# A hybrid decoder step: the sample scan's eight states in one run of TensorE passes

## The chip, the cores and the metric

The program runs on one core of one Trainium2 chip. The metric is the device time of one execution in microseconds (us): 2281.77 us before the change, the median of three runs (2281.49 to 2285.34). The engines are named as in the profile: PE is TensorE, PEld its loading of stationary operands, DVE is VectorE, ACT is ScalarE, POOL is GpSimd; SP is SyncE, which here only issues transfers.

## The reference

One inference step of a decoder layer: a SwiGLU feed-forward, a mixer, and a second feed-forward, each between RMS norms. It treats a prompt of 256 tokens with a zero initial state, and a sample group of eight sequences of four tokens, each with a stored state. The mixer has 4 GLA heads (128 keys, 256 values) and 8 HGRN heads (128 keys, 128 values). Both kinds are this recurrence, in chunks with exact causality:

```
decay  = where(causal, exp(cum_t - cum_s), 0)
scores = sum_d(q_t * k_s * decay)
o      = scores @ v + (q * exp(cum)) @ s
s_new  = exp(last) * s + (k * exp(last - cum)).T @ v
```

So a sample's output `o` has two parts: the sample's own scores times its own values, and its decayed queries times the stored state `s`. The updated states are outputs too.

## The kernel before, in words

All activations lie with features on partitions, 288 token columns to a tile: 256 of the prompt and 32 of the sample (8 sequences of 4 tokens). Weights come from HBM in units of 128x1024 floats on the SP queue (class `Weights`, lines 62 and 64), and ACT and DVE split each into a rounded part and a remainder (lines 96 and 97). Each 128x128 block of weights then makes three matmuls of 288 columns (lines 548 to 550). `block` runs through such products for 16 feature tiles `k`, and after every `k` it calls a `tick`.

The scans of the mixer live in these ticks. There are six: two for GLA and four for HGRN, with two heads each. Each is a generator (`scan`); a tick runs it on to its next `yield`, so that every step's instructions stand between the products of a weight block. The instructions of an engine keep the order that the program's planner writes out, which follows the order in the code but may move an instruction whose inputs it expects late.

A scan has nine steps (`LEVELS` + 1) that build the scores of the prompt in `Dg` and `X`, and those of the sample in `Ds` (32x32, zero between sequences). Step 3 also writes `qm[a]`: for each sequence b a block of 32 columns, which holds its four decayed queries in their places among the sample's 32 tokens and zeros elsewhere. Then come, for each head `a`:

- `out(a)`, line 1158: the prompt's output into the PSUM tile `o` (lines 1165 to 1167), three plain float32 matmuls for each 128 values; and the own-score part of the sample into the PSUM tile `os` (line 1169), values stationary (128x128) and the 32 columns of `Ds` streamed, into columns beyond the first 256.
- `sample(a, b0)`, line 1183, once for each load of states: four calls for a GLA head (`nb` = 2 sequences a load), two for an HGRN head (`nb` = 4). It computes the new states' increment in the PSUM tile `sn` (line 1191 or 1194), multiplies `qm` with each stored state (line 1198: stationary operand of 128x32, the state streamed, 256 or 128 columns) into one quarter of 32 partitions of `os`, chosen by b % 4, updates the state in place on DVE (line 1202) and stores it on POOL's queue (line 1204).
- `inter_a`, `inter_b`: the four quarters of `os` are copied to `it` and summed, turned, onto the own-score columns with the selection matrix `sel` (lines 1209 and 1214); then `norm_a` to `norm_c`.

Stored states come in through `load_state` (line 934), 256 KB a load, on the SP queue between the weights: one call in each of the steps 5 to 8 and one at the start of every `sample`. A GLA scan has eight loads, an HGRN scan four. The loads share five buffers (`bufs=5`); a buffer is free again once its updated state has been stored.

Of the kernel before, what the change touches and what calls it, by code (L numbers as in the profile page):

```python
# [9 lines left out]
F32 = mybir.dt.float32  # L10
# [6 lines left out]
P = 128  # L17
TP = 256
TS = 32
T = TP + TS  # L20
NB = 8
# [7 lines left out]
LEVELS = 8  # L29
# [96 lines left out]
def trunk_kernel(ctx, tc, x_prompt, x_sample, state_gla, state_hgrn, norm_gains, f1_in, f1_out, f2_in, f2_out,  # L126
# [3 lines left out]
    V, S, G, PE = nc.vector, nc.scalar, nc.gpsimd, nc.tensor  # L130
# [36 lines left out]
    def auxtile(name):  # L167
        return aux.tile([P, 512], F32, name=name, tag="aux")
# [607 lines left out]
    def mixer(pn, border):  # L776
        with ExitStack() as mx:
# [4 lines left out]
            sp = []  # L782
# [15 lines left out]
            its, vs32, qm = [], [], []  # L798
# [7 lines left out]
            Ds = cst.tile([P, 2, TS], F32, name="Ds")  # L806
# [48 lines left out]
            def halves(t, h, right):  # L855

                v = t[:, :, 0:T if h <= 2 else TP].rearrange("p a (n two k) -> p a n two k", two=2, k=h)
                return v[:, :, :, 1 if right else 0, :]
# [51 lines left out]
            def scan(d, Vt, V32, Vs, gla, ytile0, s0, sp_out, ss_out):  # L910
# [3 lines left out]
                dv = 256 if gla else 128  # L914
                nv = dv // P
                nb = 512 // dv
# [3 lines left out]
                fs, c = [d["f"]], 0  # L920
# [6 lines left out]
                states = {}  # L927

                def load_state():
                    if loads:  # L930
                        a, b0 = loads.pop(0)
                        t = sp[0].tile([P, nb, dv], F32, name="s0", tag="s0", bufs=5)
                        with tc.issue_after(W.last[W.loaded - 3]):
                            nc.sync.dma_start(t, s0[b0:b0 + nb, a].rearrange("b p v -> p b v"))
                        states[a, b0] = t
# [12 lines left out]
                def lay(lv, src):  # L948
                    h = 1 << lv
                    S.activation(R[:, :, lv, :].rearrange("p a (n k) -> p a n k", k=h), halves(src, h, True), AF.Copy)  # L950
# [52 lines left out]
                def update(lv, keys=None):  # L1003

                    h = 1 << lv
                    n = (T if h <= 2 else TP) // (2 * h)
                    f = fs[lv][:, :, 0:2 * n].rearrange("p a (n two) -> p a n two", two=2)
                    left, right = f[:, :, :, 0:1], f[:, :, :, 1:2]
                    if h < P and not keys:
                        v = halves(Q, h, True)  # L1010
                        V.tensor_tensor(v, v, left.broadcast_to(v.shape), op=ALU.mult)
                    if keys is not False:
                        v = halves(k, h, False)
                        V.tensor_tensor(v, v, right.broadcast_to(v.shape), op=ALU.mult)
                    if h < P and not keys:
                        V.tensor_tensor(fs[lv + 1].unsqueeze(3), left, right, op=ALU.mult)
# [12 lines left out]
                def score23():  # L1029
                    pss = [auxtile("sc23_0"), mmtile("sc23_1")]  # L1030
                    for i in range(2):
                        for a in range(2):
                            PE.matmul(pss[i][:, a * 192:(a + 1) * 192], k[:, a, i * P:(i + 1) * P],
                                      R2[0][:, :, a, i * 64:(i + 1) * 64], start=a == 0, stop=True,
                                      skip_group_check=True)
                    return pss
# [55 lines left out]
                for step in range(LEVELS + 1):  # L1092
                    if step == 0:
                        V.scalar_tensor_tensor(own.unsqueeze(3), halves(q, 1, False), 128.0, halves(k, 1, False),
                                               op0=ALU.mult, op1=ALU.mult)
                        S.activation(oh, rp, AF.Copy)
                        V.tensor_tensor(Q, q, d["f"], op=ALU.mult)
                        V.tensor_tensor(ol, rp, oh.bitcast(F32), op=ALU.subtract)
                        lay(0, q)
                    elif step == 1:  # L1100
                        update(0)
                        lay(1, Q)
                    elif step == 2:
                        pss[1] = score01()
                        update(1)
                        lay23(0)
                    elif step == 3:
                        puts = put01(*pss.pop(1))
                        update(2, False)
                        ready = lay23(1)  # L1110
                        with tc.issue_after(ready):
                            puts.pop(0)()
                    else:
                        pss[step - 1] = score23() if step == 4 else score(step - 1)
                        if step == 4:
                            update(2, True)
                        elif step == 5:
                            put23(*pss.pop(3))
                        else:
                            put(step - 2, pss.pop(step - 2))  # L1120
                        update(step - 1)
                        if puts:
                            with tc.issue_after(ready):
                                puts.pop(0)()
                    if step == 3:
                        for a in range(2):

                            S.activation(qm[a].rearrange("p (b c) -> p b c", c=TS + ST)[:, :, 0:ST],
                                         Q[:, a, TP:T].rearrange("p (b t) -> p b t", t=ST), AF.Copy)
                            S.activation(K3[:, a], k[:, a, TP:T].unsqueeze(1).broadcast_to([P, 3, TS]), AF.Copy)  # L1130
                    if step >= LEVELS - 3:
                        load_state()
                    yield
                put(LEVELS - 1, pss.pop(LEVELS - 1))
                kds, bds, sqs, pos, mss = {}, {}, {}, {}, {}
# [22 lines left out]
                def out(a):  # L1158
                    vc = Vt[:, :, a * dv:(a + 1) * dv]

                    po, ss = auxtile("o"), auxtile("os")
                    for j in range(nv):
                        vj = vc[:, :, j * P:(j + 1) * P]
                        c0, c1, c2 = j * TP, j * TP + P, (j + 1) * TP
                        PE.matmul(po[:, c0:c1], vj[:, 0, :], Dg[:, 0, a, :], start=j == 0, stop=True, skip_group_check=True)
                        PE.matmul(po[:, c1:c2], vj[:, 0, :], X[:, a, :], start=False, stop=False, skip_group_check=True)
                        PE.matmul(po[:, c1:c2], vj[:, 1, :], Dg[:, 1, a, :], start=False, stop=True, skip_group_check=True)
                        c0 = TP + j * TS
                        PE.matmul(ss[:, c0:c0 + TS], V32[:, a * dv + j * P:a * dv + (j + 1) * P], Ds[:, a, :],
                                  start=j == 0, stop=False, skip_group_check=True)  # L1170
                    pos[a] = po, ss

                def final(a):
# [9 lines left out]
                def sample(a, b0):  # L1183

                    load_state()
                    s = states.pop((a, b0))
                    ks, bd = kds[a][1], bds.pop((a, b0))
                    ps = auxtile("sn")
                    if gla:
                        for i in range(nb):  # L1190
                            PE.matmul(ps[:, i * dv:(i + 1) * dv], bd[:, i, :], Vs[:, a * dv:(a + 1) * dv],
                                      start=i == 0, stop=True, skip_group_check=True)
                    else:
                        PE.matmul(ps, ks, bd.rearrange("p b c -> p (b c)"), start=True, stop=True)
                    for i in range(nb):
                        b = b0 + i
                        r = slice(b % 4 * TS, (b % 4 + 1) * TS)
                        PE.matmul(pos[a][1][r, 0:dv], qm[a][:, b * TS:(b + 1) * TS], s[:, i, :],
                                  start=False, stop=b >= NB - 4, skip_group_check=True)
                    for i in range(nb):  # L1200
                        b = b0 + i
                        V.scalar_tensor_tensor(s[:, i, :], s[:, i, :], fs[2][:, a, 64 + b:65 + b],
                                               ps[:, i * dv:(i + 1) * dv], op0=ALU.mult, op1=ALU.add)
                    G.dma_start(ss_out[b0:b0 + nb, a].rearrange("b p v -> p b v"), s)
# [178 lines left out]
            for kind, g in HORDER:  # L1383
# [8 lines left out]
                for j in list(ds):  # L1392
                    if j // 2 in vts:
                        c = slice((j % 2) * 256, (j % 2 + 1) * 256)
# [116 lines left out]
```

## Time and profile before

| | |
|---|---|
| median of the runs | 2281.77 us |
| profiled execution | 2281.72 us, its span 2279.5 us |
| PE busy | 2265.8 us, 99% of the span |
| DVE, ACT, POOL busy | 1397.6, 1015.4, 134.6 us |
| granted clock of TensorE | 0.998 |
| DMA | 382.43 MB, mean 168 GB/s |

The scans stand in the span between about 913 and 1290 us. In the views, a row of a timeline gives the start in us from the span's start, the duration, engine, line, operation, the tiles written and read, the sizes, and how many instructions are put together in the row. A matmul `128*32 128x256` has a stationary operand of 128 rows by 32 columns and streams 256 columns. The recorded durations of matmuls overlap, since the array is pipelined. A plain float32 matmul shows as two instructions; the fp32r ones of the weight products show as one.

### The profile page before, as it was taken

How to read it: one execution, taken by the hardware profiler on the slowest of the kernel's cores; microseconds unless marked ns; L12 is line 12 of the kernel's file. 1: busy time of each engine (PE TensorE's matmuls, PEld its weight loads, DVE VectorE, ACT ScalarE, POOL GpSimd, SP SyncE). 2: the span in 40 equal slices, each digit the busy share in tenths (PEclk: the TensorE clock that was granted, in tenths of full speed). 3: DMA queues.
4: the chain of work that ended last, by engine and by line, in shares of the span. 5: the costliest groups of instructions: out<-in, count | busy, mean ns of one | idle time of the engine just before them, and what ended most of it. 6: DMA issues, size and time to landing. Idle time of an engine off the chain costs nothing.

```text
span 2279.5 us, 42047 instructions
## 1 busy us (share of the span) xinstructions
PE 2265.8 (99%) x17216; PEld 2240.5 (98%) x17216; DVE 1397.6 (61%) x2293; ACT 1015.4 (45%) x1539; POOL 134.6 (6%) x241
## 2 busy tenths in 40 slices
PE   9999999999999999999999999999999999999998
PEld 9999999999999999999999999999999999999998
DVE  7545545554555468778878754954555455545546
ACT  6443333333334346555556654644333333333344
POOL 2000000000000002001000000340000000000005
PEclk9999999999999999999999999999999999999999
DMA  7555555445555544556565554565555555455445
GB/s 218 169 167 166 167 167 165 166 165 166 166 165 184 167 158 148 165 160 186 156 172 169 160 185 158 157 191 166 167 167 166 167 167 165 164 168 165 165 164 157
DMA packets 225601, 382.43 MB, mean 168 GB/s; under 512 B 20242, under 2 KB 60224, under 8 KB 225408
## 3 DMA queue, kind: packets, MB, share of 16 engines
q1 hardware_dynamic: 214736, 365.15, 49.9%
q0 software_dynamic: 8496, 14.41, 2.3%
q8 instruction: 135, 2.21, 0.4%
q10 hardware_dynamic: 2176, 0.18, 0.1%
q14 instruction: 58, 0.48, 0.1%
HBM read 363.75 MB, written 11.80 MB: 165 GB/s over the span
## 4 chain that ended last, share of the span: by engine, by line
PE 97%; DVE 1%; ACT 0%; issue 0%; DMA 0%; DVEq 0%; SPq 0%; POOL 0%; ACTq 0%; POOLq 0%
PE gate L548 10%; PE gate L550 10%; PE gate L549 10%; PE up L550 8%; PE up L548 8%; PE up L549 8%; PE out L549 8%; PE out L550 8%; PE out L548 8%; PE mo L550 1%; PE hfq L548 1%; PE mo L548 1%; PE mo L549 1%; PE hfq L549 1%; PE hfq L550 1%; PE hi L548 1%
## 5 line engine op out<-in xcount | busy, mean ns | idle before, releaser
L97 DVE TENSOR_TENSOR wl<-raw,wh 128x1024 fp32r<-128x1024 f32 (+1 forms) x674 | 821.5, 1219 | 631.4 <-ACT wh L96 627.1
L96 ACT ACTIVATE wh<-raw 128x1024 fp32r<-128x1024 f32 (+1 forms) x674 | 711.8, 1057 | 1036.1 <-PE gate L549 318.1
L550 PE MATMUL gate<-xh,wl 128*128 128x288 f32 x1660 | 489.1, 295 | 0.5 <-DVE wl L97 0.5
L548 PE MATMUL gate<-xh,wh 128*128 128x288 f32 x1660 | 489.1, 296 | 0.1
L549 PE MATMUL gate<-xl,wh 128*128 128x288 f32 x1660 | 485.8, 295 | 0.4 <-DVE xl L255 0.4
L549 PE MATMUL out<-hl,wh 128*128 128x288 f32 x1408 | 415.6, 295 | 0.0
L550 PE MATMUL up<-xh,wl 128*128 128x288 f32 x1408 | 415.1, 295 | 0.0
L550 PE MATMUL out<-hh,wl 128*128 128x288 f32 x1408 | 415.0, 295 | 0.0
L548 PE MATMUL up<-xh,wh 128*128 128x288 f32 x1408 | 414.8, 295 | 0.0
L549 PE MATMUL up<-xl,wh 128*128 128x288 f32 x1408 | 414.6, 294 | 0.0
L548 PE MATMUL out<-hh,wh 128*128 128x288 f32 x1408 | 413.8, 294 | 0.3 <-DVE u L626 0.3
L548 PEld LDWEIGHTS gate<-xh,wh 128*128 128x128 f32 x1660 | 310.9, 188 | 1.9 <-issue 1.0
L550 PEld LDWEIGHTS gate<-xh,wl 128*128 128x128 f32 x1660 | 311.6, 188 | 1.1 <-DVE wl L97 1.0
L549 PEld LDWEIGHTS gate<-xl,wh 128*128 128x128 f32 x1660 | 310.4, 188 | 0.9 <-DVE xl L255 0.6
L548 PEld LDWEIGHTS out<-hh,wh 128*128 128x128 f32 x1408 | 264.6, 188 | 0.6 <-DVE u L626 0.6
L550 PEld LDWEIGHTS out<-hh,wl 128*128 128x128 f32 x1408 | 264.7, 188 | 0.0
L548 PEld LDWEIGHTS up<-xh,wh 128*128 128x128 f32 x1408 | 264.1, 188 | 0.4 <-ACT g L618 0.3
L549 PEld LDWEIGHTS out<-hl,wh 128*128 128x128 f32 x1408 | 264.4, 188 | 0.0
L549 PEld LDWEIGHTS up<-xl,wh 128*128 128x128 f32 x1408 | 264.2, 188 | 0.1
L550 PEld LDWEIGHTS up<-xh,wl 128*128 128x128 f32 x1408 | 264.2, 188 | 0.0
L706 DVE TENSOR_TENSOR y<-out,y 128x288 f32<-128x288 f32 x288 | 121.0, 451 | 101.3 <-PE out L550 98.3
L548 PE MATMUL hfq<-xh,wh 128*128 128x288 f32 x256 | 78.1, 305 | 0.0
(382 smaller groups left out, 2544.0 us busy)
## 6 DMA issues: line engine op xcount, KB each, us to landing
raw<-in_ffn_w_in_dram SPq DMA_DIRECT2D x351, 512.0 KB, 3.4
raw<-in_ffn_w_out_dram SPq DMA_DIRECT2D x176, 512.0 KB, 3.5
raw<-in_mix_w_in_dram SPq DMA_DIRECT2D x64, 512.0 KB, 3.7
raw<-in_mix_w_in_dram SPq DMA_DIRECT2D x96, 256.0 KB, 3.1
raw<-in_mix_w_out_dram SPq DMA_DIRECT2D x32, 512.0 KB, 3.6
out_dram<-s POOLq DMA_DIRECT2D x32, 256.0 KB, 3.1
s<-in_state_gla_dram SPq DMA_DIRECT2D x16, 256.0 KB, 4.1
s<-in_state_hgrn_dram SPq DMA_DIRECT2D x16, 256.0 KB, 5.0
```

The costliest lines, as they stand in the source:

```text
L96: i1 = self.nc.scalar.activation(h[:, c], raw[:, c], AF.Copy).ins
L97: i2 = self.nc.vector.tensor_tensor(l[:, c], raw[:, c], h[:, c].bitcast(F32), op=ALU.subtract).ins
L548: yield lambda: PE.matmul(dst, w[0][:, c:c + P], parts[0], start=start, stop=False)
L549: yield lambda: PE.matmul(dst, w[0][:, c:c + P], parts[1], start=False, stop=False)
L550: yield lambda: PE.matmul(dst, w[1][:, c:c + P], parts[0], start=False, stop=stop)
L706: V.tensor_tensor(y[k], ps, y[k], op=ALU.add)
```

## The change

All products of `qm` with the stored states move from `sample` to `out`: the eight states of a head stand one behind the other, right behind the prompt's output. The own-score product is turned round: `Ds[:, a, :]` (32 columns) is the stationary operand now and the sample's values are streamed, a quarter of their columns into each quarter of `os`, so that it adds to the same columns as the states' products and comes out of the same turn and sum in `inter_b`. `sample` keeps the increment, the update and the store. Since `out` uses all states of a head, their loads begin one step earlier, in step 4, and there are eight buffers for them.

```
-                        t = sp[0].tile([P, nb, dv], F32, name="s0", tag="s0", bufs=5)
+                        t = sp[0].tile([P, nb, dv], F32, name="s0", tag="s0", bufs=8)
...
-                    if step >= LEVELS - 3:
+                    if step >= LEVELS - 4:
                         load_state()
...
                         PE.matmul(po[:, c1:c2], vj[:, 1, :], Dg[:, 1, a, :], start=False, stop=True, skip_group_check=True)
-                        c0 = TP + j * TS
-                        PE.matmul(ss[:, c0:c0 + TS], V32[:, a * dv + j * P:a * dv + (j + 1) * P], Ds[:, a, :],
-                                  start=j == 0, stop=False, skip_group_check=True)
+
+                    for b in range(NB):
+                        r = slice(b % 4 * TS, (b % 4 + 1) * TS)
+                        PE.matmul(ss[r, 0:dv], qm[a][:, b * TS:(b + 1) * TS], states[a, b // nb * nb][:, b % nb, :],
+                                  start=b < 4, stop=False, skip_group_check=True)
+                    for i in range(4):
+                        c = slice(i * dv // 4, (i + 1) * dv // 4)
+                        PE.matmul(ss[i * TS:(i + 1) * TS, c], Ds[:, a, :], V32[:, a * dv + c.start:a * dv + c.stop],
+                                  start=False, stop=True, skip_group_check=True)
                     pos[a] = po, ss
...
                         PE.matmul(ps, ks, bd.rearrange("p b c -> p (b c)"), start=True, stop=True)
-                    for i in range(nb):
-                        b = b0 + i
-                        r = slice(b % 4 * TS, (b % 4 + 1) * TS)
-                        PE.matmul(pos[a][1][r, 0:dv], qm[a][:, b * TS:(b + 1) * TS], s[:, i, :],
-                                  start=False, stop=b >= NB - 4, skip_group_check=True)
```

## The prediction

> **What bounds the kernel.** I read the page first (busy shares, the chain that ended last), then the waits of TensorE, then its timeline in the scans, and last the SP queue and the windows.
>
> ```profile
> PE 2265.8 (99%) x17216; PEld 2240.5 (98%) x17216; DVE 1397.6 (61%) x2293; ACT 1015.4 (45%) x1539; POOL 134.6 (6%) x241
> PE 97%; DVE 1%; ACT 0%; issue 0%; DMA 0%; DVEq 0%; SPq 0%; POOL 0%; ACTq 0%; POOLq 0%
> PE sc L1067 <- DVE k_g L1014: 0.3, 1, 0.3
> ```
>
> TensorE is busy for 99% of the span and carries 97% of the chain; its longest wait for another engine in a scan is 0.3 us. So TensorE's own instruction stream is the bound, and what counts of a matmul is how long it keeps the next one from starting: the distance between two starts, not the 0.3 us that one lasts. Next, a GLA `sample` in the stream of weight products; the columns are start, duration, what, and how many.
>
> ```profile
> 960.95 0.29 PE L549 MATMUL v<-xl,wh 128*128 128x288 f32 x1
> 961.08 0.30 PE L550 MATMUL v<-xh,wl 128*128 128x288 f32 x1
> 961.22 0.40 PE L1191 MATMUL sn<-Vsg,bd 96*128 96x256 f32 x2
> 961.55 0.63 PE L1198 MATMUL os<-s,qm 128*32 128x256 f32 x4
> 962.10 0.40 PE L548 MATMUL v<-xh,wh 128*128 128x288 f32 x1
> 962.34 0.29 PE L549 MATMUL v<-xl,wh 128*128 128x288 f32 x1
> ```
>
> A weight product costs 0.13 us. The 32-column passes (`os<-s,qm`, 128*32) break the rhythm twice: they start 0.33 - 0.13 = 0.20 us after the second `sn` matmul, and after them the first 128-column product holds the stream for 0.24 us. A plain float32 matmul shows as two instructions, so x4 is two states.
>
> ```profile
> L1198 PE MATMUL os<-s,qm x192: 272/297/404, 949.5 to 1277.7; 128*32 128x128 f32 x128, 128*32 128x256 f32 x64
> 1023.17 0.64 PE L1198 MATMUL os<-s,qm 128*32 128x256 f32 x8
> 1023.74 0.40 PE L548 MATMUL hi<-xh,wh 128*128 128x288 f32 x1
> ```
>
> Here the passes of two samples happen to stand together: x8 takes 0.57 us to the next product, where x4 took 0.55. Four states on four quarters cost what two on two quarters cost: the quarters work side by side. The counts give the number of runs: GLA 64 / 4 = 16, two of them merged, so 15; HGRN 128 / 8 = 16.
>
> **Removed: the runs inside `sample`.** GLA: from the first `sn` to the second weight product is 962.34 - 961.22 = 1.12 us. Without the run there are three steps of 0.13 (a 256-column `sn` is no longer than a 288-column product), 0.39. That is 0.73 saved, x15 = 10.95 us. For HGRN the trace has `sn` without a run behind it, and with one:
>
> ```profile
> 1275.47 0.40 PE L1194 MATMUL sn<-bd,ks 96*128 96x512 f32 x1
> 1275.71 0.30 PE L549 MATMUL gate<-xl,wh 128*128 128x288 f32 x1
> ```
>
> ```profile
> 1277.17 0.40 PE L1194 MATMUL sn<-bd,ks 96*128 96x512 f32 x1
> 1277.50 0.43 PE L1198 MATMUL os<-s,qm 128*32 128x128 f32 x8
> 1277.85 0.41 PE L548 MATMUL gate<-xh,wh 128*128 128x288 f32 x1
> 1278.10 0.30 PE L549 MATMUL gate<-xl,wh 128*128 128x288 f32 x1
> ```
>
> With it 0.93 us to the second product, without it 0.24 + 0.13 = 0.37: 0.56 saved, x16 = 8.96 us. Removed in all: 19.9 us.
>
> **Added: one longer run in `out`, in place of the `os<-Ds,vs` products.** The end of `out` today, in an HGRN head, and its middle in a GLA head:
>
> ```profile
> 1085.79 0.39 PE L1167 MATMUL o<-Dg,Vh 128*128 128x128 f32 x2
> 1086.02 0.31 PE L1169 MATMUL os<-Ds,vs 128*128 128x32 f32 x2
> 1086.16 0.38 PE L548 MATMUL hfq<-xh,wh 128*128 128x288 f32 x1
> 1086.38 0.29 PE L549 MATMUL hfq<-xl,wh 128*128 128x288 f32 x1
> ```
>
> ```profile
> 1017.44 0.39 PE L1167 MATMUL o<-Dg,Vg 128*128 128x128 f32 x2
> 1017.66 0.31 PE L1169 MATMUL os<-Ds,vs 128*128 128x32 f32 x2
> 1017.80 0.47 PE L1165 MATMUL o<-Dg,Vg 128*128 128x128 f32 x2
> 1018.11 0.39 PE L1166 MATMUL o<-rp,Vg 128*128 128x128 f32 x2
> ```
>
> HGRN after: a pair of 128-column float32 instructions takes 0.22 (1017.44 to 1017.66), so the second one of `L1167` starts at 0.11, and the run 0.20 after that: 0.31. The x8 row has two rounds over four quarters and its leaving: 1278.10 - 1277.50 = 0.60. Eight states are four rounds, so two more of 0.11 (one 128-column instruction): 0.22. Then the sample's own scores, two rounds of 32 streamed columns. Nearest is a run of 32-column passes that comes back to the same two quarters eight times:
>
> ```profile
> 1077.05 0.45 PE L1063 MATMUL sc<-Q,k_h 128*32 128x32 f32 x16
> 1077.43 0.40 PE L550 MATMUL hfq<-xh,wl 128*128 128x288 f32 x1
> ```
>
> 0.38 us for eight rounds with the leaving: under 0.05 a round. I take 0.03, with 0.11, a whole 128-column instruction, as the upper end: 0.06. Sum 0.31 + 0.60 + 0.22 + 0.06 = 1.19, against 0.59 today (1085.79 to 1086.38): +0.60, x8 heads = 4.8 us.
>
> GLA after: 0.31, then the x4 row up to its second product (961.55 to 962.34, two rounds) 0.79, two more rounds of 0.22 (twice the columns of an HGRN round) 0.44, the own scores at twice the columns 0.12: 1.66. Today the end is as in HGRN, 0.59, and the first `L1169` pair costs 1018.11 - 1017.44 = 0.67 where two pairs alone take 0.44: 0.23 more. So +0.84, x4 heads = 3.4 us.
>
> Sum: -19.9 + 4.8 + 3.4 = -11.7 us. With the own scores at their upper end (0.11 a round in HGRN, 0.22 in GLA) it is 8x0.16 + 4x0.32 = 2.6 us less.
>
> **Moved: who waits.** `out` now needs all eight states of the head at once; `sample` needed one load at a time. Behind a late load stands the whole weight stream. Rows of the SP queue, of the tile `s` and of TensorE:
>
> ```profile
> 937.42 0.47 SPq L934 DMA_DIRECT2D s<-in_state_gla_dram  x1
> 948.95 0.57 PE L1191 MATMUL sn<-Vsg,bd 96*128 96x256 f32 x2
> 967.13 0.37 SPq L934 DMA_DIRECT2D s<-in_state_gla_dram  x1
> 970.02 0.38 PE L1165 MATMUL o<-Dg,Vg 128*128 128x128 f32 x2
> SPq L934 <- DMA out_dram<-s: 20.4, 6, 5.7
> DMA to landing us min/median/max: 2.5/3.7/7.7
> 1241.47 1.57 SPq L934 DMA_DIRECT2D s<-in_state_hgrn_dram  x3
> 1253.86 0.38 PE L1165 MATMUL o<-Dg,Vh 128*128 128x128 f32 x2
> ```
>
> The last HGRN scan issues its loads 12 us ahead of its `out`; even 7.7 us lands in time. The tight place is the second head of the first GLA scan: its last load goes out at 967.13, and the run would begin at about 970.02 - 4x0.73 + 0.84 + 1.5 (six pairs of 0.22 and 0.20) = 969.5. A landing of 3.7 us would be 1.4 late, 7.7 us 5.3 late. But the queue issues that load late because it waits for stores to give buffers back (six times, 20.4 us), which eight buffers end, and the load moves one `sample` earlier. Between 0 and 5 us for each GLA scan I take 0.5 us in all, near zero, by the load that waits for no buffer: emitted with the first `sample`, it went out at 937.42, 11.5 us ahead of that sample's `sn` at 948.95.
>
> The first load of each scan one step earlier puts 256 KB ahead of weights in SP's queue; hidden, since TensorE waits for no weights there. The in-place update of `s` on DVE stands behind `sn` alone now; DVE isn't the bound, so nothing is booked.
>
> The profiled execution took 2281.72 us (span 2279.5); the median of the runs is 2281.77. So 2281.7 - 11.7 + 0.5 = 2270.5 us, 0.5% faster. About 0.2%, 4.6 us, is the least that a measurement of this kernel tells from no change.
>
> **A rule against it.** The x8 rows show rounds of four quarters, the x16 row rounds of two, 0.11 us or less apart. The Trainium skill, TensorE: Matmul & The Clock Gate, section Part 3: Packing small matmuls, says that matmuls start and end strictly in program order. Taken literally, the second instruction of one float32 matmul, on the same quarter as the first, would hold up the next quarter. This trace does not bear that out for four states; no row has eight.
>
> **The rivals.**
> (1) *The long run doesn't pack.* Coming back to a quarter costs as if each state took its two instructions alone: four more rounds, 8x0.44 + 4x0.88 = 7.0 us; gain 4.2, 2277.5. For it: no row has eight states. Against: the x16 row revisits quarters without a gap. The skill's rule above would lead here.
> (2) *The planner cuts the run* at the state loads. A cut costs the broken rhythm, 0.56 - 2x0.11 = 0.34. GLA in four pieces: 3x0.34 and four rounds of 0.22 lost, x4 = 7.6 us; HGRN in two: 8x0.34 = 2.7. Gain 11.2 - 10.3 = 0.9, 2280.8; with half of the cuts 2275.7. For it: each load has its own landing, and the planner may move what waits for one. Against: the loads are issued early.
> (3) *DVE becomes the wait* in the HGRN scans, and their share (8.96 - 4.8 = 4.2 us) is lost: 2274.7.
>
> ```profile
> 1160.00:1225.00 65.00, 65.00 (x524) 62.30 (x524) 56.87 (x128) 42.21 (x95) 4.17 (x6) 1.00 0.60 169
> ```
>
> Its columns are the stretch, its length, then PE, weight loads, DVE: 56.87 of 65 us, 87%. Against: a scan's two heads save 1 us in 65, which leaves DVE under 90%.
> (4) *Slower: TensorE waits for states at the run.* Place: the first passes of each of the 12 runs. If loads went out as `out` is reached, each would cost a landing, 12x3.7 = 44 us, less 11.7: 2314. It decides from 11.7 / 12 = 1 us a head. For it: all states are wanted at once, in a queue shared with weights. Against: the 12 us and 11.5 us above.
>
> **Chances.** Forecast 0.76; (1) 0.04; (2) 0.08, half of it with a gain over 4.6 us; (3) 0.06; (4) 0.06. Faster 0.76 + 0.04 + 0.06 = 0.86; same 0.04 + 0.04 = 0.08; slower 0.06. The forecast's own bounds are 2269 (no wait, runs a little shorter) to 2274 (own scores at the upper end, a late load); the range goes 2 us below for what else the planner moves, and up to rival (3) and half of (2): 2267 to 2277.
>
> **What would show it.** Right: 12 runs instead of 31, x24 each, and nothing of 128*32 behind `sn`; from a run's start to the next product about 0.65 us (HGRN) and 1.1 us (GLA); no wait of SP for `out_dram<-s`; the stretch from 945 to 1290 shorter by about 11 us and the others equal. Wrong: idle time of TensorE before `os` that a DMA of `s` ends; runs in pieces or longer than that; `sn` waiting for the update of `s` on DVE.

## The result and the profile after

The changed kernel takes 2272.1 us (median of four runs, 2271.3 to 2273.22) against 2282.2 us before: a ratio of 0.9952, 95% interval 0.9938 to 0.9966, so 10.1 us or 0.5% faster. The prediction was 2270.5 us, 2267 to 2277.

The page of the changed kernel, its busy shares and its chain, and two rows of the tile `os`:

```profile
PE 2256.4 (99%) x17280; PEld 2240.9 (99%) x17280; DVE 1395.4 (61%) x2293; ACT 1014.4 (45%) x1539; POOL 134.7 (6%) x241
PE 96%; DVE 1%; DMA 1%; issue 1%; ACT 1%; POOL 0%; DVEq 0%; SPq 0%; ACTq 0%; POOLq 0%
L1171 PE MATMUL os<-s,qm x192: 272/285/403, 949.4 to 1258.1; 128*32 128x128 f32 x128, 128*32 128x256 f32 x64
L1175 PE MATMUL os<-vs,Ds x96: 192/196/219, 950.3 to 1258.2; 128*32 128x32 f32 x64, 128*32 128x64 f32 x32
```

TensorE is the bound as before, with more instructions (17280 against 17216) in less time. Its timeline shows the new run in a GLA head, and then in an HGRN head:

```profile
970.70 0.39 PE L1167 MATMUL o<-Dg,Vg 128*128 128x128 f32 x2
971.01 1.07 PE L1171 MATMUL os<-s,qm 128*32 128x256 f32 x16
971.90 0.29 PE L1175 MATMUL os<-vs,Ds 128*32 128x64 f32 x8
972.13 0.40 PE L548 MATMUL v<-xh,wh 128*128 128x288 f32 x1
972.37 0.29 PE L549 MATMUL v<-xl,wh 128*128 128x288 f32 x1
...
1080.11 0.39 PE L1167 MATMUL o<-Dg,Vh 128*128 128x128 f32 x2
1080.43 0.65 PE L1171 MATMUL os<-s,qm 128*32 128x128 f32 x16
1080.89 0.24 PE L1175 MATMUL os<-vs,Ds 128*32 128x32 f32 x8
1081.07 0.40 PE L548 MATMUL hfq<-xh,wh 128*128 128x288 f32 x1
1081.30 0.30 PE L549 MATMUL hfq<-xl,wh 128*128 128x288 f32 x1
```

The start-to-start reading gives 1.12 us from the run to the next product in GLA (971.01 to 972.13) and 0.64 us in HGRN (1080.43 to 1081.07). From `L1167` to the second product it is 1.67 and 1.19 us; the prediction had worked out 1.66 and 1.19. A GLA `sample` is now only its two `sn` matmuls, 0.24 us in the stream:

```profile
962.29 0.40 PE L1197 MATMUL sn<-Vsg,bd 96*128 96x256 f32 x2
962.53 0.30 PE L548 MATMUL v<-xh,wh 128*128 128x288 f32 x1
962.67 0.29 PE L549 MATMUL v<-xl,wh 128*128 128x288 f32 x1
```

**Where the time went.** Both kernels make the same weight products in the same order, so one can take the start of the same product in both traces. These are the 2301st, 2501st and 3001st product of line 548: ahead of the first `out`, between the GLA and the HGRN scans, and behind the last scan. First the timeline of the kernel before, then of the changed one:

```profile
943.21 0.38 PE L548 MATMUL qk<-xh,wh 128*128 128x288 f32 x1
...
1060.16 0.38 PE L548 MATMUL hfq<-xh,wh 128*128 128x288 f32 x1
...
1315.07 0.29 PE L548 MATMUL gate<-xh,wh 128*128 128x288 f32 x1
```

```profile
944.67 0.38 PE L548 MATMUL qk<-xh,wh 128*128 128x288 f32 x1
...
1054.44 0.38 PE L548 MATMUL hfq<-xh,wh 128*128 128x288 f32 x1
...
1306.51 0.29 PE L548 MATMUL gate<-xh,wh 128*128 128x288 f32 x1
```

From first to last it is 371.86 us before and 361.84 after: 10.0 us, the whole gain, of which GLA has 116.95 - 109.77 = 7.2 and HGRN 254.91 - 252.07 = 2.8. The changed kernel's profiled execution was 1.46 us behind at the first of these products, and already 1.52 us at the 200th product of the line (92.94 us against 91.42), in a part that the change doesn't touch; that is most of why the two spans (2279.5 and 2271.3) differ by only 8.2. Every trace below is read over the same products; the stretch is far steadier than the times.

| kernel | median us | ratio to before, 95% | GLA us | HGRN us | both us |
|---|---|---|---|---|---|
| before | 2282.2 | | 116.95 | 254.91 | 371.86 |
| changed | 2272.1 | 0.9952 (0.9938 to 0.9966) | 109.77 | 252.07 | 361.84 |
| loads only | 2282.53 | 1.0001 (0.9991 to 1.0010) | 116.95 | 254.91 | 371.86 |
| five buffers | 2276.83 | 0.9974 (0.9963 to 0.9985) | 112.01 | 252.11 | 364.12 |
| same quarter next | 2273.51 | 0.9958 (0.9941 to 0.9974) | 109.85 | 252.23 | 362.08 |
| values stationary | 2275.37 | 0.9970 (0.9959 to 0.9981) | 110.82 | 252.73 | 363.54 |
| run cut once | 2276.94 | 0.9976 (0.9966 to 0.9987) | 111.16 | 254.15 | 365.31 |
| GLA only | 2275.51 | 0.9972 (0.9960 to 0.9983) | 109.81 | 254.94 | 364.75 |
| both heads in one run | 2271.68 | 0.9951 (0.9939 to 0.9964) | 109.79 | 250.70 | 360.50 |
| changed, again | 2273.46 | 0.9959 (0.9946 to 0.9973) | 109.81 | 252.09 | 361.90 |

### The profile page after: what moved, and what is told of

It reads as the page before. It is cut to its first block, busy times and chain, and to the rows that moved or that the text cites. A ratio compares the mean times of both kernels' runs of the same rounds, so it can differ in the third digit from the quotient of the medians.

```text
span 2271.3 us, 42178 instructions
## 1 busy us (share of the span) xinstructions
PE 2256.4 (99%) x17280; PEld 2240.9 (99%) x17280; DVE 1395.4 (61%) x2293; ACT 1014.4 (45%) x1539; POOL 134.7 (6%) x241
## 4 chain that ended last, share of the span: by engine, by line
PE 96%; DVE 1%; DMA 1%; issue 1%; ACT 1%; POOL 0%; DVEq 0%; SPq 0%; ACTq 0%; POOLq 0%
PE gate L548 10%; PE gate L550 10%; PE gate L549 10%; PE out L549 8%; PE out L550 8%; PE out L548 8%; PE up L550 8%; PE up L548 8%; PE up L549 8%; PE mo L550 1%; PE mo L548 1%; PE mo L549 1%; PE hfq L548 1%; PE hfq L549 1%; PE hfq L550 1%; PE hi L548 1%
```

## The experiments

The theory is that TensorE's stream alone explains the gain: fewer changes between 128-column and 32-column passes, and in GLA all four quarters filled in place of two. Rivals are that the loads or the buffers made it, and that a run of eight states is held up by the order of its instructions.

**The loads alone.** The kernel before, with eight buffers and the first load a step earlier:

```
-                        t = sp[0].tile([P, nb, dv], F32, name="s0", tag="s0", bufs=5)
+                        t = sp[0].tile([P, nb, dv], F32, name="s0", tag="s0", bufs=8)
-                    if step >= LEVELS - 3:
+                    if step >= LEVELS - 4:
                         load_state()
```

> The kernel before with only the loads changed: eight buffers, first load in step 4; all products stay where they were. Stream theory (the gain is the time TensorE loses at changes between 32-column and 128-column passes): no gain, 2281 to 2283 us, the wait of SP for out_dram<-s (20.4 us) gone all the same, 31 runs of x4 or x8. Loads theory (the gain comes from SP no longer waiting, so that weights or states are earlier): most of the 10 us, 2272 to 2275 us.

No gain: the ratio is 1.0001, and the stretch (from 945.67 to 1317.53 in this trace) is 371.86 us as before, to the hundredth. SP no longer waits for `out_dram<-s` at all, and that is worth nothing by itself. The loads theory falls.

**Five buffers again.** The other way round: the changed kernel with `bufs=5`.

> The changed kernel with five buffers for the states again. Stream theory: the runs keep their length (1.11 and 0.64 us to the next product), but the second head of each GLA scan has to wait for loads that wait for stores: TensorE idle before os, ended by a DMA of s, 1 to 5 us in each of two places, 2273 to 2282 us; HGRN scans unchanged. If the buffers don't matter (the planner finds other work, or the loads land in time): 2271 to 2273 us with no such idle time.

Rows of its waits (SP's, then of the loading of stationary operands), and of its timeline in the second head of the second GLA scan:

```profile
SPq L934 <- DMA out_dram<-s: 18.8, 5, 4.9
PEld os L1171 <- DMA s<-in_state_gla_dram: 2.0, 2, 1.6
```

```profile
1038.93 1.06 PE L1171 MATMUL os<-s,qm 128*32 128x256 f32 x12
1041.07 0.41 PE L1171 MATMUL os<-s,qm 128*32 128x256 f32 x2 [1.08 <-DMA s<-in_state_gla_dram]
1041.08 0.30 PE L1175 MATMUL os<-vs,Ds 128*32 128x64 f32 x4
1041.31 0.39 PE L1171 MATMUL os<-s,qm 128*32 128x256 f32 x2
1041.52 0.28 PE L1175 MATMUL os<-vs,Ds 128*32 128x64 f32 x4
1041.74 0.40 PE L548 MATMUL hi<-xh,wh 128*128 128x288 f32 x1
```

The run takes 2.81 us in place of 1.11: its last load (x2 and x2, the last two states) isn't there. The other waiting run, in the second head of the first GLA scan, takes 1.65. That is 1.7 + 0.5 us, the second less than the 1 us expected; the stretch is 2.3 us longer, all of it in GLA. So the eight buffers bring nothing alone, and without them over a fifth of the gain is lost: with them `out` can ask for all states at once and not wait. The prediction had named the first GLA scan's second head as the tight place; the longer wait came at the same place of the second scan. Both lie inside its 0 to 5 us.

**Neighbours on the same quarter.**

```
-                    for b in range(NB):
+                    for b in (0, 4, 1, 5, 2, 6, 3, 7):
```

> The changed kernel with the states taken in the order 0, 4, 1, 5, 2, 6, 3, 7, so that two neighbours in the program share a quarter. If matmuls start strictly in program order, a quarter's four instructions hold up the next quarter: about 12 to 16 steps of 0.11 us in a run in place of four, run starts to the next product about 1.5 us (HGRN) and 2.8 us (GLA), 12 to 15 us slower than the changed kernel, 2284 to 2288 us. If the quarters are filled independently of the program's order: no change, 0.64 and 1.11 us, 2271 to 2274 us.

```profile
1079.48 0.67 PE L1171 MATMUL os<-s,qm 128*32 128x128 f32 x16
1079.94 0.26 PE L1175 MATMUL os<-vs,Ds 128*32 128x32 f32 x8
1080.14 0.40 PE L548 MATMUL hfq<-xh,wh 128*128 128x288 f32 x1
```

The run takes 0.66 us in place of 0.64, although the built program has states 0, 4, 1, 5 in this order and each pair shares a quarter. The starts of the first four quarters stand 13 ns apart instead of 7, and that is all. The quarters are filled side by side in this order too; the rule of the Trainium skill that the prediction weighed (TensorE: Matmul & The Clock Gate, Part 3: Packing small matmuls, matmuls strictly in program order) is not borne out by this run for passes on different quarters.

**The own scores as before.**

```
+                        c0 = TP + j * TS
+                        PE.matmul(ss[:, c0:c0 + TS], V32[:, a * dv + j * P:a * dv + (j + 1) * P], Ds[:, a, :],
+                                  start=j == 0, stop=False, skip_group_check=True)
...
-                    for i in range(4):
-                        c = slice(i * dv // 4, (i + 1) * dv // 4)
-                        PE.matmul(ss[i * TS:(i + 1) * TS, c], Ds[:, a, :], V32[:, a * dv + c.start:a * dv + c.stop],
-                                  start=False, stop=True, skip_group_check=True)
```

> The changed kernel with one part undone: the own scores with the values as stationary operand (128x128) and Ds streamed, as before, ahead of the run; the run is x16. Stream theory: two instructions of 0.11 us for each 128 values come back (0.22 in an HGRN head, 0.45 in a GLA head), and two rounds of the run go (0.07 and 0.12): 8x0.15 + 4x0.33 = 2.5 us slower than the changed kernel, 2273.5 to 2276 us. If turning the own scores is worth nothing or is the main part of the gain: 2272 us, or over 2278 us.

```profile
1080.15 0.39 PE L1167 MATMUL o<-Dg,Vh 128*128 128x128 f32 x2
1080.37 0.31 PE L1169 MATMUL os<-Ds,vs 128*128 128x32 f32 x2
1080.61 0.64 PE L1174 MATMUL os<-s,qm 128*32 128x128 f32 x16
1081.18 0.40 PE L548 MATMUL hfq<-xh,wh 128*128 128x288 f32 x1
```

From `L1167` to the next product it is 1.03 us against 0.96 in the changed kernel: the pair brings 0.14 more before the run (0.46 from `L1167` to the run against 0.32), and the run is 0.07 shorter (0.57 against 0.64). The stretch is 1.7 us longer, 1.05 in GLA and 0.66 in HGRN, less than the 2.5 expected. Turning the own scores round is the small part of the change, 1.7 of 10 us.

**The run cut once.** The last product of the prompt's output goes between the first and the last four states:

```
+                    for j in range(nv):
+                        prompt(j, 0)
+                        if j < nv - 1:
+                            prompt(j, 1)
+                    four(0)
+                    prompt(nv - 1, 1)
+                    four(4)
```

> The changed kernel with each head's run cut once: the last product of the prompt's output (two 128-column instructions) stands between the first four and the last four states. All quarters stay filled and no work is added. Stream theory with the price from the prediction (0.34 us for a broken rhythm): 24 pieces instead of 12, x8 and x16, 12x0.3 to 12x0.4 = 3.7 to 4.8 us slower than the changed kernel, 2275.5 to 2277.5 us. If the changes between column widths cost little and the gain comes from elsewhere (no wait of DVE behind os, fewer instructions): 2272 us.

```profile
1083.14 0.42 PE L1174 MATMUL os<-s,qm 128*32 128x128 f32 x8
1083.50 0.49 PE L1169 MATMUL o<-Dg,Vh 128*128 128x128 f32 x2
1083.92 0.43 PE L1174 MATMUL os<-s,qm 128*32 128x128 f32 x8
1084.16 0.24 PE L1186 MATMUL os<-vs,Ds 128*32 128x32 f32 x8
1084.33 0.40 PE L548 MATMUL hfq<-xh,wh 128*128 128x288 f32 x1
```

Eleven runs are cut; the planner closed the twelfth again. The stretch is 365.31 - 361.84 = 3.5 us longer, a little under the 3.7 to 4.8 expected for twelve cuts, and 0.31 us for each cut, with no work added and every round still full. This measures one more change of width, there and back, by itself; the prediction had 0.34.

**GLA alone.** HGRN scans as before, GLA as changed, loads as changed:

```
+                    if gla:
+                        for b in range(NB):
...
+                    for i in range(0 if gla else nb):
```

> The changed kernel with the HGRN scans as before (values stationary, products with the states in sample), the loads as in the changed kernel. By the prediction GLA carries 10.95 - 3.4 = 7.5 of 11.7 us; by the trace of the changed kernel 7.2 of 10. So 7 us faster than before, 2275 us, with 4 runs of x24 and 16 of x8. If DVE or the planner had taken part of the HGRN scans' gain, their start-to-start sums here would differ from those of the kernel before; if the parts don't add up, over 2278 or under 2273 us.

2275.51 us; GLA 109.81 us as in the changed kernel, HGRN 254.94 as in the kernel before (254.91). The parts add up, 7.1 and 2.9 us, and neither takes from the other. The HGRN scans lost nothing to DVE: TensorE's longest wait for it in a scan of the changed kernel is 0.3 us, as before. They did lose a little to two new waits for ACT, which this run doesn't have; they are shown further down, with the prediction.

**Both heads of an HGRN scan in one run.** The price of a change suggests fewer of them still. Head 1's states go into columns 128 to 255 of the same PSUM tile, in head 0's `out`:

```
+                    heads = [a] if gla else [0, 1] if a == 0 else []
+                    for h in heads:
+                        o0 = 0 if gla else h * dv
+                        for b in range(NB):
```

> The changed kernel with the runs of the two heads of an HGRN scan put together in the first head's out: x48, head 1 in columns 128 to 255 of the same PSUM tile; its out keeps only the prompt's products. 4 GLA runs of x24 and 4 HGRN runs of x48, 8 instead of 12. By the rows of the changed kernel, a run costs 0.20 us to enter and 0.24 - 0.13 us in the first product behind it beside its rounds, and an end of out without a run costs 0.33 us: 1.08 - 0.33 - 0.51 = 0.24 us saved for each of four scans, 1 us in all, too little for the times; the scan stretch of the trace should be shorter by 0.8 to 1.2 us. If the second head's loads come too late for the earlier run: TensorE idle before os, and no gain.

```profile
1081.04 1.08 PE L1175 MATMUL os<-s,qm 128*32 128x128 f32 x32
1081.94 0.31 PE L1181 MATMUL os<-vs,Ds 128*32 128x32 f32 x16
1082.18 0.40 PE L548 MATMUL hfq<-xh,wh 128*128 128x288 f32 x1
```

One run of 1.14 us in place of two of 0.64. The HGRN stretch is 250.70 us, 1.4 us shorter than in the changed kernel (252.07, and 252.09 in its repeat), more than the 0.8 to 1.2 expected. Not all of it comes from the grouping: the score products of lines 958 and 1033 take 8.10 us of the stream in place of 8.31, and `sn` waits for ACT once in place of twice, 0.2 us each; that leaves about 0.9 us. The times, 2271.68 us and 2273.46 for the repeat on the same chip, point the same way, but their intervals overlap; the trace alone shows this gain.

**The changed kernel again.**

> The changed kernel once more, for comparison on the same chip: 12 runs of x24, 9.5 to 10.5 us between the kernel before and this one in the scan stretch of the trace, 2271 to 2273 us. The beginning of the program, which the change does not touch, differs from run to run in the traces by up to 2 us, and should do so again.

2273.46 us, and the stretch 361.90 us, 0.06 from the first trace. The first of the three products stood at 944.54; over all traces here it lies between 943.21 and 946.20, in a part of the program that no edit touches.

## Why the prediction was right

**The bound.** Right: the gain is 10.0 us in TensorE's stream between the first `out` and the last scan, and nothing elsewhere.

**Removed and added.** GLA was forecast at 15x0.73 - 4x0.84 = 7.6 us and gave 7.2. HGRN was forecast at 16x0.56 - 8x0.60 = 4.2 and gave 2.8. The added run is right in both (1.66 and 1.19 forecast, 1.67 and 1.19 measured). The mis-sized term is the saving for an HGRN `sample`: with the added run as forecast it is (2.84 + 4.8) / 16 = 0.48 in place of 0.56. Three things make about 1.0 of the missing 1.3 us.

First, the 0.56 had been read at one place where a weight product follows. In four of the sixteen a plain float32 transposition follows. Such a place before, and the same one after:

```profile
1090.65 0.40 PE L1194 MATMUL sn<-bd,ks 96*128 96x512 f32 x1
1090.98 0.43 PE L1198 MATMUL os<-s,qm 128*32 128x128 f32 x8
1091.34 0.44 PE L866 MATMUL tp_k<-ident,k_h 128*128 128x128 f32 x2
...
1091.64 0.38 PE L548 MATMUL hfq<-xh,wh 128*128 128x288 f32 x1
```

```profile
1085.03 0.40 PE L1200 MATMUL sn<-bd,ks 96*128 96x512 f32 x1
1085.26 0.38 PE L866 MATMUL tp_k<-ident,k_h 128*128 128x128 f32 x2
...
1085.51 0.38 PE L548 MATMUL hfq<-xh,wh 128*128 128x288 f32 x1
```

0.99 us against 0.48, so 0.51 saved, 0.05 less than forecast; over four places that is 0.2 us.

Second, in the changed kernel `sn` itself waits at two places, and the prediction had no term for this. A row of the waits of the loading of stationary operands, and the timeline at one of the two:

```profile
PEld sn L1200 <- ACT st L1186: 0.4, 2, 0.2
```

```profile
1129.72 0.29 PE L549 MATMUL hfq<-xl,wh 128*128 128x288 f32 x1
1129.97 0.50 PE L1200 MATMUL sn<-bd,ks 96*128 96x512 f32 x1
1130.31 0.29 PE L550 MATMUL hfq<-xh,wl 128*128 128x288 f32 x1
```

The weight product ahead holds the stream for 0.25 us in place of 0.13, and `sn` for 0.34 in place of 0.24. The other place, at 1267.65, is alike: 0.46 us in both. The profile puts the wait down to ACT's copy of the prompt's new state `st`. The repeat of the changed kernel has the same two waits, the kernel before and the one with GLA alone have none; why `sn` comes to depend on that copy was not tested.

Third, the score products of lines 958 and 1033 in the HGRN scans take 8.31 us of the stream in place of 7.98, summed from start to start: 0.33 us. The planner placed some of them otherwise; in one scan two groups of four stand six weight products apart, which had stood one apart.

The remaining 0.3 us or so was not traced to single rows.

That the time came within 1.6 us of the forecast has some luck in it: the saving in the stream was forecast 1.7 us too large (11.7 against 10.0), and 0.5 us booked for waits on states, which did not come, hid a part of that.

**Own scores.** Two rounds of 0.03 us a head were right; `L1175` adds 0.07 in HGRN by the runs with and without it (0.64 and 0.57).

**Who waits.** Right, and shown from both sides: no TensorE wait for a state with eight buffers, 2.3 us with five, at the two second heads of GLA. The 0.5 us that were booked for this did not come. SP's waits with a state load are, in the changed kernel, this one row; none is for `out_dram<-s`:

```profile
SPq L934 <- PE qk L550: 0.5, 1, 0.5
```

One reading was off without consequence: the landing of 3.7 us is the median over the loads and the stores of `s` together. The page of the kernel before gives 4.1 us for the GLA loads alone and 5.0 for the HGRN loads.

**The rivals.** (1), the long run that doesn't pack, is refuted by the rows of the run and by the changed order. (2): the planner kept all twelve runs whole (192 and 96 instructions in twelve runs of x24); the price for a cut, 0.34, measured 0.31. (3), DVE as the new wait, did not appear: the longest wait of TensorE for DVE in a scan is 0.3 us, as before. The small new waits are for ACT. (4) has its mechanism, seen with five buffers, but at two heads and not at twelve.

## What to carry to other kernels

When TensorE is the bound, cost a matmul by the distance to the next start, and count the changes between column widths: here each break of the stream, there and back, costs 0.31 us beyond its work, about as much as two and a half weight products of 0.13 us. Group narrow passes so that one entry serves many, and fill all four quarters in it. The operands must then all be there at once; give the loads buffers enough before moving the work, since the buffers bring nothing alone but decide whether the grouped run waits. And look for new waits afterwards: here `sn` waited for ACT at two places, which the forecast had no term for.

## What the runs showed of the hardware

Passes on different quarters ran side by side even with two neighbours in the program on the same quarter (0.66 us against 0.64 for 24 instructions). And TensorE's stream in an undisturbed stretch repeats almost exactly: 371.86 us in two kernels whose loads differ, 361.84 and 361.90 us for the changed one, while the whole times of one kernel spread over 2 us and more. Effects of 1 us, which the times can't tell, can be read by comparing the starts of the same products.
